# Sixteen of 22 input units as seven half-size products each (Strassen), in two passes over K, with the combinations and all stages through DRAM

## The chip, the cores and the metric

The kernel runs on one core of a Trainium2 chip. The metric is the time of the whole execution on the device in microseconds, the median over several runs of the same program. All tensors come from DRAM and the result goes back to it. Everything below is float32; a product of two float32 matrices is made from rounded high parts and remainders, as told below.

## The reference, cut to what matters

One pre-norm mixer layer of a hybrid encoder on x of 1024 tokens and 2048 columns:

```python
h = rmsnorm(x, norm_w)                       # 1024 x 2048
proj = einsum('bsd,de->bse', h, w_in)        # 2048 x 5632 input weights
q_a, k_a, v_a, g_a, q_r, k_r, v_r, g_r = split(proj)
# widths: 1024, 256, 256, 1024,  512, 512, 1024, 1024
attn = windowed_attention(q_a, k_a, v_a, sink, rel_bias)   # 16 heads of 64, 4 KV heads, +-128 tokens
attn = rmsnorm(attn, attn_out_norm_w) * silu(g_a)
ret = bidirectional_retention(rotary(q_r), rotary(k_r) * 64**-0.5, v_r, ...)   # 8 heads, chunks of 128
ret = head_groupnorm(ret, ret_gn_w) * silu(g_r)
x = x + einsum('bse,ed->bsd', concat(attn, ret), w_out)    # 2048 x 2048
return rmsnorm(x, final_norm_w)
```

The two projections are most of the arithmetic. Attention looks at bands of three 128-token blocks, with a learned sink and a relative-position bias; retention runs a scan over chunks of 128 tokens in each direction.

## The kernel before, in words

**Products.** [...] A product is three matmuls into one accumulator: high by high, high by low, low by high.

**Units.** The 5632 input columns are cut into 22 units of 256 columns, named for what they hold: "ka" and "va" (attention keys and values), four each of "qa" (queries), "ga" and "gr" (gates of attention and retention), "qk" (retention queries and keys) and "vr" (retention values). A unit takes 16 k-steps of 128 rows of the 2048; a step multiplies into four accumulators "psM" of 128 columns by 512 tokens (L817 to L819, 128x512 matmuls). In "va" and "vr" the result is wanted with tokens on the partitions: eight 128x256 products a step (L810 to L812). So a unit is 192 wide matmuls, or 384 of half the width. The normalised input lies in SBUF as hT, 32 rows of 128x1024: for each k-step a high and a low row. It holds x times the norm weight; the factor 1/rms per token is put on when an accumulator is taken out (evac, with the tile "rb" or the column "rcol").

**Weights.** One transfer of 256 KB brings two k-steps ("wr", two buffers). ScalarE casts the high part "wh" (L105), GpSimd subtracts for the low part "wl" (L99; VectorE in the output phase). Each has two buffers, and a pair feeds 24 matmuls.

**Side work.** After each three matmuls point() may advance two queues of generators: `jobs` holds attention (160 steps, in four groups) and retention (four jobs of two heads), `aux` the set-up: sums of squares, the bias rows, decay factors, gates and rotary factors after their units. The bias rows are copied by DMA sixteen times from "br" to "bd" through the shared tiles t (t2, 6 buffers), right after they have been computed. Attention and retention results go to DRAM "md", gates after their tanh to "gd"; before the output projection mixed_row loads a row, scales it and splits it into hT.

**Output.** Eight units (two halves of the tokens, four blocks of 512 columns) multiply hT by w_out, 192 matmuls each (L899 to L901); the last has its weights in the free part of hT already.

**Order.** The program emits instructions as these loops run, and a scheduler then sets the order on each engine, so an engine's order is read from the compiled program. An engine works off its own order and waits on semaphores. All loads and stores are issued by SyncE (SP), each one only after the one eight places earlier has landed.

## Time and profile before

| | us |
|---|---|
| time, median of 3 runs (lowest, highest) | 1581.26 (1580.31, 1585.71) |
| the profiled execution: its time | 1581.46 |
| its span, first instruction to last | 1579.7 |
| TensorE busy | 1539.7 (97%) |
| VectorE busy | 798.9 (51%) |
| ScalarE busy | 525.2 (33%) |
| GpSimd busy | 414.1 (26%) |
| bytes over DMA | 171.76 MB, mean 109 GB/s |

Mean granted TensorE clock 0.994 of full speed.

Engines are named PE (TensorE), DVE (VectorE), ACT (ScalarE), POOL (GpSimd) and SP (SyncE, which issues transfers). A row of the view by stretches is: the stretch in us after the span's start and its length; busy us of PE (and number of matmuls, as x192), then of the weight loads of PE, of DVE, ACT and POOL; the granted TensorE clock as a share of full speed; the mean busy share of the 16 DMA engines and the GB/s they moved. A row of the groups is: line, engine, operation, output tile and inputs, shape, count | busy us, mean ns of one | idle us of the engine right before them, and which instruction's end finished most of that idle time. A row of the chain of waits is a time, a length and the work that released the next. A row of the DMA issues ends with the KB of one and the median us from issue to landing. "PE psT L502 <- DVE PTl L99: 4.0, 9, 1.2" in the view of waits is: who waits for whom, us in all, how often, the longest.

A busy TensorE is the usual state of this program. The input units run from 6.2 to 1216.7 us, the output units from there to 1570; the rest is the last rows' norm and stores.

### The profile page before, as it was taken

What the parts mean: (1) busy time and instruction counts of PE and PEld (TensorE: products, weight loads), DVE (VectorE), ACT (ScalarE), POOL (GpSimd) and SP (SyncE); (2) the same over time, 40 slices, a digit from 0 to 9 for tenths busy, and PEclk for the clock granted to TensorE, in tenths of its full rate; (3) what the DMA queues carried; (4) which work ended last, traced back from release to release, by engine and by line L of the source; (5) the groups of instructions that cost most, each with busy time, mean ns of one, the idle gap of its engine ahead of it and who ended that gap; (6) DMA issues with size and microseconds to landing.
All of it is one profiled execution on the core that took longest, in us unless ns stands there. A gap on an engine that the chain in (4) does not pass through costs nothing.

```text
span 1579.7 us, 22620 instructions
## 1 busy us (share of the span) xinstructions
PE 1539.7 (97%) x8338; PEld 1327.6 (84%) x8338; DVE 798.9 (51%) x1888; ACT 525.2 (33%) x1186; POOL 414.1 (26%) x435
## 2 busy tenths in 40 slices
PE   8979999999999999999999999999999999999997
PEld 6968888888888888888998998998988888888886
DVE  5511156644656478466534825735567463463323
ACT  5412145543554356456410111111123243433310
POOL 2212223332334334334331423323322000320000
PEclk9989999999999999999999999999999999999999
DMA  8774313131213123212231321312222565675423
GB/s 299 246 248 125 104 43 92 51 114 45 84 56 114 48 60 94 73 48 83 54 113 41 107 61 50 111 41 67 88 89 91 186 205 151 180 247 139 127 61 113
DMA packets 111020, 171.76 MB, mean 109 GB/s; under 512 B 17932, under 2 KB 39436, under 8 KB 110781
## 3 DMA queue, kind: packets, MB, share of 16 engines
q1 hardware_dynamic: 110908, 170.32, 35.3%
q8 instruction: 65, 1.06, 0.3%
q14 instruction: 47, 0.38, 0.1%
HBM read 138.26 MB, written 32.01 MB: 108 GB/s over the span
## 4 chain that ended last, share of the span: by engine, by line
PE 82%; DVE 8%; DMA 4%; issue 3%; ACT 1%; POOL 1%; SPq 0%; POOLq 0%; ACTq 0%; DVEq 0%
PE psM L817 14%; PE psM L818 14%; PE psM L819 14%; PE psM L811 3%; PE psM L812 3%; PE psM L810 3%; PE psM L900 3%; PE psM L901 3%; PE psM L899 3%; PE psT L502 2%; DMA t<-br 1%; DVE t L102 1%; PE psS L900 1%; PE psS L899 1%; PE psS L901 1%
## 5 line engine op out<-in xcount | busy, mean ns | idle before, releaser
L817 PE MATMUL psM<-hT,wh 128*128 128x512 f32 x1088 | 443.0, 407 | 14.9 <-ACT t L741 8.7
L819 PE MATMUL psM<-hT,wl 128*128 128x512 f32 x1088 | 425.9, 392 | 2.0 <-POOL wl L99 2.0
L818 PE MATMUL psM<-hT,wh 128*128 128x512 f32 x1088 | 426.2, 392 | 0.0
L99 POOL TENSOR_TENSOR wl<-wr,wh 128x512 fp32r<-128x512 f32 x176 | 234.5, 1333 | 583.7 <-ACT wh L105 570.7
L105 ACT CAST wh<-wr 128x512 fp32r<-128x512 f32 x288 | 178.5, 620 | 568.7 <-PE psM L818 226.4
L817 PEld LDWEIGHTS psM<-hT,wh 128*128 128x128 f32 x1088 | 205.7, 189 | 53.6 <-ACT t L741 8.9
L819 PEld LDWEIGHTS psM<-hT,wl 128*128 128x128 f32 x1088 | 204.9, 188 | 47.3 <-POOL wl L99 2.4
L818 PEld LDWEIGHTS psM<-hT,wh 128*128 128x128 f32 x1088 | 206.1, 189 | 37.5 <-DVE hT L102 0.7
L810 PE MATMUL psM<-wh,hT 128*128 128x256 f32 x640 | 183.5, 287 | 1.4 <-ACT wh L105 1.4
L811 PE MATMUL psM<-wl,hT 128*128 128x256 f32 x640 | 181.9, 284 | 2.4 <-POOL wl L99 2.4
L812 PE MATMUL psM<-wh,hT 128*128 128x256 f32 x640 | 181.8, 284 | 0.0
L99 DVE TENSOR_TENSOR wl<-wr,wh 128x512 fp32r<-128x512 f32 x112 | 84.1, 751 | 130.8 <-ACT wh L105 130.7
L811 PEld LDWEIGHTS psM<-wl,hT 128*128 128x128 f32 x640 | 123.4, 193 | 3.0 <-POOL wl L99 2.8
L810 PEld LDWEIGHTS psM<-wh,hT 128*128 128x128 f32 x640 | 123.5, 193 | 2.5 <-ACT wh L105 1.6
L812 PEld LDWEIGHTS psM<-wh,hT 128*128 128x128 f32 x640 | 123.4, 193 | 0.0
L450 DVE CUSTOM_DVE_ANT_0 P<-psS,bias,nsink 128x384 f32<-128x384 f32 (+1 forms) x128 | 74.3, 580 | 91.7 <-PE psS L444 91.3
L454 ACT ACTIVATE P<-P,nmx 128x384 f32<-128x384 f32 (+1 forms) x128 | 75.6, 590 | 92.1 <-DVE nmx L450 90.7
L900 PE MATMUL psM<-wl,hT 128*128 128x512 f32 x256 | 100.0, 391 | 0.6 <-DVE wl L99 0.5
L899 PE MATMUL psM<-wh,hT 128*128 128x512 f32 x256 | 100.0, 391 | 0.0
L901 PE MATMUL psM<-wh,hT 128*128 128x512 f32 x256 | 99.7, 389 | 0.0
L99 POOL TENSOR_TENSOR acc<-acc,sq 64x128 f32<-64x128 f32 x112 | 54.9, 490 | 156.2 <-ACT sq L483 148.1
L99 DVE TENSOR_TENSOR t<-psM,rb 128x512 f32<-128x512 f32 x64 | 42.2, 685 | 93.4 <-PE psM L819 93.2
(200 smaller groups left out, 2259.6 us busy)
## 6 DMA issues: line engine op xcount, KB each, us to landing
wr<-in_w_in SPq DMA_DIRECT2D x176, 256.0 KB, 2.7
wr<-in_w_out SPq DMA_DIRECT2D x112, 256.0 KB, 2.8
t<-in_x SPq DMA_DIRECT2D x16, 512.0 KB, 6.9
mr<-md SPq DMA_DIRECT2D x32, 256.0 KB, 3.0
xr<-in_x SPq DMA_DIRECT2D x32, 256.0 KB, 3.9
out<-y SPq DMA_DIRECT2D x32, 256.0 KB, 3.0
t<-in_xT SPq DMA_DIRECT2D x15, 512.0 KB, 5.8
gd<-t SPq DMA_DIRECT2D x28, 256.0 KB, 2.4
```

Source lines behind the costliest of these rows:

```text
L99: eng.tensor_tensor(o, x, y, op)
L105: A.copy(o_hi, x)
L454: A.activation(x[:, :W], x[:, :W], AF.Exp, bias=nmx[:, c : c + 1], scale=-1.0, accum_out=sums[:, c : c + 1])
L810: T.matmul(po, hh[:, sl], wh[:, ws], start=first and z == 0, stop=False, skip_group_check=True)
L811: T.matmul(po, hh[:, sl], wl[:, ws], start=False, stop=False, skip_group_check=True)
L812: T.matmul(po, hl[:, sl], wh[:, ws], start=False, stop=last, skip_group_check=True)
L817: T.matmul(p, wh[:, ws], hh[:, sl], start=first, stop=False)
L818: T.matmul(p, wh[:, ws], hl[:, sl], start=False, stop=False)
L819: T.matmul(p, wl[:, ws], hh[:, sl], start=False, stop=last)
L899: T.matmul(p, mh, wh, start=(k == 0), stop=False)
L900: T.matmul(p, mh, wl, start=False, stop=False)
L901: T.matmul(p, ml, wh, start=False, stop=(k == NK - 1))
```

## The change

**Sixteen units as Strassen products.** "ka", "va" and the four "qa" stay as they were and come first (STD). The other sixteen (FAST) are taken as block products in Strassen's form with Winograd's sums: K is cut into two passes of 1024 rows, and in each pass a unit's weights (1024 x 256) and the input (1024 tokens) are seen as 2x2 blocks. Seven products of half-size blocks replace eight, so a unit and pass takes 7 x 4 x 3 = 84 matmuls of 128x512 (L953 to L955) instead of 96. No unit of FAST has tokens on the partitions now: "vr" is transposed afterwards, four 128x128 transposes a block, 64 in all (L1035).

**The input's combinations.** The seven left-hand combinations of the input are the same for all units. combine() makes them in the side queue during the standard units: it loads blocks of x again, normalises them fully, forms sums, splits each into a tile "crow" (128x1024, two buffers) and stores it to DRAM "cd", 28 rows of 512 KB for each pass. Standard units still use the first form of hT. The 28 rows of the first pass are loaded into hT during the last standard unit (whose k-steps run 14, 15, 0 to 13, so that rows come free early), those of the second when the pass changes.

**The weights' combinations.** w_fast holds the weights in blocks. prep() loads four 256 KB blocks for a unit and pass, VectorE forms two sums and GpSimd two more, and each of the seven is split as before (ScalarE cast, GpSimd low part) two products ahead of its use, with three buffers for each part.

**The results' combinations.** Products accumulate in "psMa" and "psMb", two banks each. collect() copies the partial sums of bank a out between products that go on adding to it, by ScalarE in the first pass and VectorE in the second. The first pass's four results of a unit go to DRAM "yd" and come back to be added in the second. deliver() then makes the gates, rotary products or token-order values of a result and stores them to DRAM, from where retention and mixed_row load them.

**What else moves.** Queries are split and staged through DRAM "qsd" for attention. Copies of the bias rows are cut in groups of four: the first stands behind combine(0) in the side queue, three in the last standard unit. The gates are multiplied in mixed_row, for eight of the sixteen rows with one more operation on GpSimd. A step of attention or retention is taken each 3.1 calls of point(), later each 4.2 (before: 3), and one of the side queue each 2.0, later 2.4 (before: 2).

```diff
+STD = [("ka", 0), ("va", 0), ("qa", 0), ("qa", 1), ("qa", 2), ("qa", 3)]
+FAST = []
 for _p in range(4):
-    UNITS += [("qk", _p), ("vr", _p)]
+    FAST += [("qk", _p), ("vr", _p)]
+FAST += [(_k, _p) for _k in ("ga", "gr") for _p in range(4)]
...
+    def combine(ph):
+        for j in range(4):
+            b = [stp.tile([128, 512], F32, tag=f"b{x}", name=nm("b"), bufs=1) for x in range(4)]
+            for x in range(4):
+                k = 8 * ph + 4 * (x // 2) + j
+                SP.dma_start(b[x], a["xT"][k][:, 512 * (x % 2) : 512 * (x % 2) + 512])
+            yield
+            yield
+            for x in range(4):
+                k = 8 * ph + 4 * (x // 2) + j
+                stt(V, b[x], b[x], nw[:, k : k + 1], rb[x % 2], ALU.mult, ALU.mult)
+            b11, b12, b21, b22 = b
+            def row(p, t):
+                c = stp.tile([128, 1024], F32R, tag="crow", name=nm("crow"), bufs=2)
+                split(c[:, 0:512], c[:, 512:1024], t, G if p % 2 else V)
+                SP.dma_start(cd[ph, 4 * p + j], c.bitcast(F32))
+            row(0, b11)
+            yield
+            tt(V, b11, b12, b11, ALU.subtract)
+            row(3, b11)
+            yield
...
+    aux.append((combine(0), None))
+    aux.append((bias_copies(0), None))
+    aux.append((combine(1), None))
+    aux.append((decay(), None))
...
+            k = (pos + 14) % NK if last_u else pos
...
+            if last_u and pos >= 4:
+                for r in range(2 * pos - 8, 2 * pos - 6):
+                    c_load(0, r)
...
+    def prep(q, p):
...
+        elif p == 2:
+            s1, s2 = rt(F32), rt(F32)
...
+            tt(V, s1, w(2), w(3), ALU.add)
+            tt(V, s2, s1, w(0), ALU.subtract)
+            src = s2
...
+        hi, lo = wpair(q)
+        split(hi, lo, src, G)
...
+    def multiply(q, p):
+        if p in (0, 1, 3):
+            banks[q, "abc"[(0, 1, 3).index(p)]] = psum("Ma" if p == 0 else "Mb", 2)
+        bank = banks[q, {0: "a", 2: "a", 4: "a", 5: "a", 1: "b", 3: "c", 6: "c"}[p]]
...
+        for j in range(4):
...
+            hh, hl = hT[:, 4 * p + j, 0:512], hT[:, 4 * p + j, 512:1024]
+            T.matmul(bank, wh[:, ws], hh, start=(j == 0 and p in (0, 1, 3)), stop=False, skip_group_check=True)
+            T.matmul(bank, wh[:, ws], hl, start=False, stop=False, skip_group_check=True)
+            T.matmul(bank, wl[:, ws], hh, start=False, stop=(j == 3), skip_group_check=True)
+            point()
+    def partial(q, b):
+        if (q, b) not in outs:
+            outs[q, b] = et_(("e11", "e12", "e21", "e22")[b])
+            if q >= NF:
+                SP.dma_start(outs[q, b], yd[q - NF, b])
+        return outs[q, b]
+    def collect(q, p):
...
+        def take(b, bank):
+            o = partial(q, b)
+            if ph:
+                tt(V, o, bank, o, ALU.add)
+            else:
+                A.copy(o, bank)
+            return o
+        if p == 0:
+            take(0, ba)
+        elif p == 1:
+            tt(V, outs[q, 0], bb, outs[q, 0], ALU.add)
+            deliver(q, 0)
+        elif p == 2:
+            take(1, ba)
...
+    for q in range(2 * NF):
+        slots.append((q, 0))
+        if q:
+            slots.append((q - 1, 5))
+        slots.append((q, 1))
+        if q:
+            slots.append((q - 1, 6))
+        slots += [(q, 2), (q, 3), (q, 4)]
...
+    for n, (q, p) in enumerate(slots):
+        if n + 2 < len(slots):
+            prep(*slots[n + 2])
...
+        multiply(q, p)
...
+        collect(q, p)
...
+        if old:
+            pp = old.popleft()
+            for j in range(4):
+                c_load(1, 4 * pp + j)
+        if q == NF - 1:
+            old.append(p)
```

Three places show how instructions moved. Rows name the line, the operation, the output tile and its inputs, and the shape; "x2" stands for two in a row.

ScalarE in the standard units, before: behind the two copies of "rb" (the 1/rms factors) its weight casts "wh" follow one another, with a few small set-up operations.

```order
L130 COPY rb<-psS_660 128x512
L130 COPY rb<-psS_666 128x512
L304 ACTIVATE lu_1029<-lz_1030 128x24
L105 CAST wh_741<-wr_676 128x512
L318 ACTIVATE cdec<-lg_1033 128x16
L321 ACTIVATE kdec<-kdec 128x16
L105 CAST wh_807<-wr_745 128x512
L105 CAST wh_873<-wr_811 128x512
```

The same engine there in the changed program; "crow" are the combined rows, "b" the blocks they are cast from, "e" the tiles that now hold raw weights.

```order
L120 CAST crow_804<-b_756 128x512
L120 CAST wh_837<-e_111_774 128x512
L120 CAST crow_827<-b_756 128x512
L120 CAST crow_850<-b_757 128x512
L120 CAST crow_867<-b_756 128x512
L120 CAST wh_909<-e_116_841 128x512
L337 ACTIVATE lu_2092<-lz_2093 128x24
L120 CAST crow_889<-b_759 128x512
L120 CAST crow_905<-b_758 128x512
L120 CAST wh_976<-e_123_913 128x512
```

Two or three casts of combined rows now stand ahead of each weight cast.

SP in the middle of attention, before: one weight load at a time, between the attention's stores and loads.

```order
L143 DMA wr_4133<-in_w_in 128x512
L493 DMA md<-u_4077 64x2x128
L509 DMA gt_4182<-gd 64x2x128
L143 DMA wr_4202<-in_w_in 128x512
L493 DMA md<-u_4168 64x2x128
L509 DMA gt_4264<-gd 64x2x128
L143 DMA wr_4281<-in_w_in 128x512
```

SP at the end of the last standard unit, in the changed program; "r" are the raw weight blocks of the first products.

```order
L465 DMA qj_2941<-qsd 64x2x256 x2
L544 DMA md<-u_2951 64x2x128
L810 DMA hT<-cd 128x1024 x2
L286 DMA bd<-t_494_2925 128x512
L909 DMA r_3010<-in_w_fast 128x512
L909 DMA r_3012<-in_w_fast 128x512
L909 DMA r_3014<-in_w_fast 128x512
L909 DMA r_3016<-in_w_fast 128x512
L810 DMA hT<-cd 128x1024 x4
L909 DMA r_3039<-in_w_fast 128x512
L909 DMA r_3041<-in_w_fast 128x512
```

The first products' weights stand behind 24 row loads of hT, and the bias copies to "bd" are now among them.

ScalarE in the densest attention, before:

```order
L513 CAST PTh_3895<-psT_3932 128x3x128
L454 ACTIVATE P_3923,sums_3870<-P_3923,nmx_3869 128x384
L457 ACTIVATE esk_3871<-esk_3871 128x2
L105 CAST wh_3948<-wr_3861 128x512
L454 ACTIVATE P_3966,sums_3964<-P_3966,nmx_3963 128x256
L479 COPY sq_3982<-psO_3974 64x256
L513 CAST PTh_3994<-psT_3990 128x3x128
```

The same engine in the first pass of the changed program; "e" are partial sums taken out of "psMa".

```order
L507 ACTIVATE P_4555,sums_4506<-P_4555,nmx_4505 128x256
L510 ACTIVATE esk_4507<-esk_4507 128x2
L977 COPY e_905_4573<-psMa_4211 128x512
L120 CAST wh_4577<-r_4306 128x512
L532 COPY sq_4605<-psO_4597 64x256
L507 ACTIVATE P_4594,sums_4592<-P_4594,nmx_4591 128x384
L536 ACTIVATE sq_4605<-u_4604 64x256
L560 CAST PTh_4615<-psT_4612 128x2x128
L120 CAST wh_4627<-r_4296 128x512
L977 COPY e_920_4625<-psMa_4581 128x512
```

A weight cast stands there for each product of 12 matmuls, and copies of the banks stand between them.

668 lines of the change are left out of this document (395 added, 273 removed).

## The prediction

> **What bounds the kernel now.** I read the head of the page first, then its chain of waits, then busy time in stretches cut at the boundaries of units.
>
> ```profile
> span 1579.7 us, 22620 instructions
> PE 1539.7 (97%) x8338; PEld 1327.6 (84%) x8338; DVE 798.9 (51%) x1888; ACT 525.2 (33%) x1186; POOL 414.1 (26%) x435
> PE 82%; DVE 8%; DMA 4%; issue 3%; ACT 1%; POOL 1%; SPq 0%; POOLq 0%; ACTq 0%; DVEq 0%
> ...
> 160.49:204.01 43.52, 43.52 (x193) 36.04 (x192) 5.96 (x9) 8.31 (x15) 10.33 (x8) 1.00 0.31 94
> 1308.41:1351.93 43.52, 43.52 (x194) 36.04 (x193) 15.80 (x25) 13.61 (x27) 0.00 (x0) 1.00 0.48 130
> 935.19:994.34 59.15, 59.05 (x314) 49.44 (x313) 31.14 (x83) 6.87 (x12) 15.97 (x15) 1.00 0.18 55
> 994.34:1044.03 49.69, 49.69 (x417) 49.58 (x416) 25.64 (x63) 6.97 (x12) 15.78 (x11) 1.00 0.29 90
> 52.20:114.40 62.20, 51.19 (x404) 49.59 (x402) 20.04 (x51) 12.56 (x26) 11.88 (x9) 0.93 0.69 224
> 114.40:160.50 46.10, 46.10 (x192) 37.91 (x193) 8.36 (x29) 10.02 (x26) 10.31 (x8) 0.94 0.47 138
> ```
>
> TensorE is 82% of the chain. The first two stretches are one input unit and one output unit: 192 matmuls of 128x512 in 43.52 us, nothing lost, at full clock (1.00). So a matmul costs 0.2267 us, and the 30 units' worth (22 input, 8 output) cost 1305.6 of the span's 1579.7 us. The other 274.1 us are the attention and retention matmuls between them, the start, the tail, and one loss: the unit "va" (52.2 to 114.4) leaves TensorE idle for 11.0 us, and half-clock time makes the next unit 2.6 us long (46.10 against 43.52).
>
> **The floor of the change.** Sixteen input units become 2 passes x 16 units x 7 products x 12 matmuls = 2688 of the same 128x512 form, against 16 x 192 = 3072: two units fewer, 87.0 us. The loss in "va" goes:
>
> ```profile
> 84.37 5.39 DMA t<-br
> ...
> 108.70 4.60 DMA bd<-t
> 113.48 0.85 ACT t L741 x2
> 114.37 0.80 PE psM L817
> ...
> L652 PE MATMUL psT<-ident,on 128*128 128x128 f32 x64 | 9.9, 275 | 0.0
> ```
>
> These chain pieces show it: the evacuation waits for buffers that the copies of the bias rows hold. The change queues these copies behind the first combinations, so 11.0 + 2.6 = 13.6 us go. Added are 64 transposes of the values "vr" to token order; the same number of retention transposes (last row, of the groups by line) is busy 9.9 us. Against that, four "vr" units drop their 256-wide matmuls: 994.34 to 1044.03 has 49.69 us with 32 small retention matmuls, which at 0.13 us each (15.6 us over 43.52 for some 121 of them in 935.19 to 994.34) are 4.2, leaving 1.9 over 43.52, 7.6 for four. Floor: 1579.7 - 87.0 - 13.6 + 9.9 - 7.6 = 1481.4 us, if nothing new makes TensorE wait. Attention and retention keep their matmuls.
>
> **What the change adds, and what hides it.** The transfers of the program grow from 170.3 to 314.5 MB, counted from the rows of the order. These are the rates and latencies to hold against it:
>
> ```profile
> 6.20:52.20 46.00, 45.96 (x192) 37.19 (x193) 27.00 (x29) 26.24 (x31) 11.58 (x8) 1.00 0.92 332
> 30.00:45.00 15.00, 15.00 (x68) 12.43 (x67) 7.33 (x9) 8.68 (x11) 4.51 (x3) 1.00 0.96 343
> 45.00:60.00 15.00, 15.00 (x99) 13.75 (x97) 8.88 (x12) 6.80 (x12) 2.58 (x2) 1.00 0.98 343
> 1340.00:1395.00 55.00, 55.00 (x245) 45.53 (x244) 23.40 (x25) 24.04 (x45) 19.38 (x15) 1.00 0.61 182
> ...
> gd<-t SPq DMA_DIRECT2D x28, 256.0 KB, 2.4
> t<-in_xT SPq DMA_DIRECT2D x15, 512.0 KB, 5.8
> wr<-in_w_in SPq DMA_DIRECT2D x176, 256.0 KB, 2.7
> ...
> DMA to landing us min/median/max: 2.9/4.1/5.3
> ...
> L105 ACT CAST wh<-wr 128x512 fp32r<-128x512 f32 x288 | 178.5, 620 | 568.7 <-PE psM L818 226.4
> L99 POOL TENSOR_TENSOR wl<-wr,wh 128x512 fp32r<-128x512 f32 x176 | 234.5, 1333 | 583.7 <-ACT wh L105 570.7
> L99 DVE TENSOR_TENSOR wl<-wr,wh 128x512 fp32r<-128x512 f32 x112 | 84.1, 751 | 130.8 <-ACT wh L105 130.7
> L99 DVE TENSOR_TENSOR t<-psM,rb 128x512 f32<-128x512 f32 x64 | 42.2, 685 | 93.4 <-PE psM L819 93.2
> ```
>
> The stretches are in us, with the DMA engines' share and GB/s at the end; the issues show the median us to landing. The queues are full at 343 GB/s (shares 0.96 and 0.98).
>
> *Combinations, standard units, +18.* In the order, ScalarE casts 56 rows "crow" among 28 weight casts. A weight tile feeds 24 matmuls, 5.44 us, so a row has 2.72 us before TensorE waits: the weight cast stands behind it in ScalarE's order. A row needs its cast (0.62), the low part (0.75 on VectorE for four of seven, 1.33 on GpSimd for three, mean 1.0, 1.1 with a semaphore or two) and its 512 KB store. There are two buffers. The only 512 KB store in the trace is that of rbd; that tile's three transfers landed after 2.9, 4.1 and 5.3 us, and 4.1 is the middle one: (0.62 + 1.1 + 4.1) / 2 = 2.9 us a row, 0.18 x 56 = 10 us late. Lower bound: landing after 2.4 us (gd<-t, half the size), nothing late. Upper bound: 5.8 us (t<-in_xT, in a full queue), 3.76 us a row, 58 us late. The same stretch of SP's order moves 51.9 MB in 28 x 5.44 = 152 us of TensorE work, and at 343 GB/s that takes 151 us. A queue that may never pause, on which stores wait for compute, will pause: I add 8, for 18 in all.
>
> *Into the first pass, +5.* During the last standard unit SP's order holds 22.0 MB, 64 us at 343 GB/s. The unit is 43.5 us plus 24 attention steps at 0.8, 62.9 us (0.8: in 204 to 772 stand ten units, 435 of 568 us; less the idle 6.1 shown below, 127 us for some 157 steps). The first product's weights are queued behind 24 row loads and need 2.7 + 0.62 + 1.33 us more, of which two positions of the unit, 7.8 us, give cover. Bounds 0 and 12 (cover gone); 5 lies nearer the queue's own 1 us.
>
> ```profile
> 204.00:480.00 276.00, 273.56 (x1377) 232.57 (x1377) 156.63 (x413) 130.70 (x341) 94.33 (x111) 1.00 0.25 70
> 480.00:655.30 175.30, 172.57 (x883) 145.08 (x881) 107.79 (x274) 88.30 (x234) 69.07 (x90) 1.00 0.29 81
> 655.30:772.00 116.70, 115.79 (x598) 98.98 (x598) 77.19 (x209) 62.94 (x168) 42.19 (x54) 1.00 0.21 62
> ...
> PE psT L502 <- DVE PTl L99: 4.0, 9, 1.2
> ```
>
> *First pass, +8.* Before, TensorE idles 2.4 + 2.7 + 0.9 us through all of attention, and the longest wait for a low part there is 1.2 us (last row's third number). Now one bank of four partial sums is copied out between products, twice per unit with a single product (2.72 us and its share of attention) between copy and next write: 32 spots. VectorE goes from 107.8 / 175.3 = 61% to at most 88% (9 steps x 2.2, from 341.6 us in 157 steps with all evacuations, plus five ops at 0.7, in 19.0 + 7.2 us). Bounds 0 and 32 x 1.2 = 38; a quarter of a microsecond per spot is 8. The weight splits (0.62, then 1.33) run two products ahead and stay covered; without that cover each product would be 2 us late.
>
> *Between passes, +10.* All 28 rows of hT are loaded again, 19.7 MB from the first to the last row load in SP's order: 57 us at 343 GB/s, against 16 products with what is left of attention, 43.5 + 12.6 = 56 us. But a product's rows cannot be asked for before it is done, so in the first three slots only one seventh of it can be on its way: some 8 us of rate lost. Bounds 0, and 25 at 298 GB/s (182 / 0.61, the 2 KB rows of the fourth line above) with that loss.
>
> *Second pass, +10.* VectorE now takes the copies itself (13 ops a unit or less beside ropes), each after a reload of its partial sum, while retention runs: 56.8 us per job (31.14 + 25.64, ropes in it) over 4.2 units, 13.5, plus 6.3, in 19.0 + 5.2 us: 82%. Same 32 spots, same bounds, a little more.
>
> *Last products, +4.* Fourteen rows of mixed input are split there by VectorE (0.75 and one more op each), some 21 us in 24.5 us that also hold retention; before, a whole unit covered it. Bounds 0 and 15.
>
> Sum: 18 + 5 + 8 + 10 + 10 + 4 = 55, so a span of 1536. The profiled execution took 1581.46 us with its span of 1579.7, 1.8 more, and lies 0.2 from the median of the runs, 1581.26. Forecast: **1538 us**.
>
> [...]
>
> **The rivals.** *The transfers keep ahead:* row loads and stores that have no compute behind them overlap, store landings are nearer 2.4 than 4.1, and only waits for banks and the last products stay, 4 + 5 + 4: 1481.4 + 13 + 1.8 = 1496. For it: 332 GB/s were held through the first unit (6.20 to 52.20) with TensorE busy. Against it: those were loads into five buffers, not stores from two. [...]
>
> *No change:* the two passes are bound by banks and VectorE; 32 spots at about 1 us in each pass, 30 + 35, with the other terms as above (37): 1481.4 + 102 + 1.8 = 1585. For it: 82 to 88% on an engine that serves in order. Against it: the densest attention before, at 61%, lost 2.7 us in 175.
>
> *Slower:* one mechanism, the two-buffer store of combined rows inside the standard units. If a 512 KB store lands as the 512 KB loads did at the start, 5.8 us, the term is 58, and the same full queue gives both passes' row loads their upper bounds, 12 and 25: with 8 + 10 + 4, 1481.4 + 117 + 1.8 = 1600. With those loads it decides from (98.3 - 59) / 56 = 0.70 us over 2.72, a row cycle of 3.4 us, which is a landing of 5.1 us.
>
> That the change doesn't do what it says I exclude: the order holds the 2688 matmuls.
>
> **How the numbers follow.** Forecast 0.50 (its own range 1515 to 1562), transfers ahead 0.22, no change 0.12, slower 0.16. A difference of 0.3%, 4.7 us, is what these runs can tell. Of "no change" I give 0.04 to faster, 0.06 to same, 0.02 to slower. Faster 0.76, same 0.06, slower 0.18. The range of 1488 to 1595 holds the forecast and no change whole and most of the first rival (1488 is 5 over the floor's 1483), and leaves out slower.
>
> **What would show it.** For the floor: a fast product without attention in 2.72 us, and the gap in "va" gone. For the combinations: the page's GB/s near 300 through the standard units, casts of "crow" idle behind its store, and units there some 6 us over 43.5. For the passes: two dips in TensorE, at the last standard unit and in the middle of the products. Waits of TensorE on ScalarE (first pass) or VectorE (second) before the third and fifth product would be the bank spots. Wrong is the forecast if store landings stay under 3 us, if the longest waits stand in the passes' steady part, or if fast products run well over 2.72 us without a wait.

## The result: slower by 7%, and the profile after

The changed kernel takes 1691.86 us (median of 4 runs, 1689.79 to 1698.35), the kernel before 1582.98 beside it: a ratio of 1.0695, 95% interval 1.0659 to 1.0731. The forecast was 1538, its range 1488 to 1595. The profiled execution took 1689.79 us with a span of 1688.0.

The head of the page of the changed kernel, and its chain of waits by engine:

```profile
span 1688.0 us, 22276 instructions
PE 1513.9 (90%) x7250; PEld 1242.1 (74%) x7250; DVE 1040.6 (62%) x2082; ACT 636.4 (38%) x1368; POOL 663.9 (39%) x587
...
PE 40%; DVE 19%; DMA 12%; POOL 9%; issue 7%; ACT 5%; SPq 2%; POOLq 0%; ACTq 0%; DVEq 0%
```

The matmuls did become fewer: 7250 rows for 8338, though TensorE's busy time fell by only 26 us. TensorE was 82% of the chain and is 40%; VectorE, transfers and GpSimd have taken its place.

Busy time in stretches of the changed kernel, cut at the five standard units before the last, the last standard unit, the first pass, the first three units of the second, the rest of it to its last unit, that unit with the first output unit, and the other output units. The expectations below call the units of both passes f0 to f31 and the output units o0 to o7: the first pass is f0 to f15, the joint of the passes f16 to f18, and f19 to f31 is the second pass up to its last unit.

```profile
6.50:273.40 266.90, 237.76 (x1171) 198.86 (x1171) 151.37 (x219) 94.24 (x156) 90.03 (x64) 0.95 0.78 272
273.40:369.50 96.10, 76.77 (x339) 57.87 (x340) 47.34 (x143) 42.43 (x117) 14.60 (x17) 0.90 0.93 305
369.50:829.30 459.80, 422.58 (x2145) 349.96 (x2144) 318.81 (x731) 262.71 (x667) 244.31 (x255) 1.00 0.44 134
829.30:911.80 82.50, 72.90 (x328) 58.72 (x327) 45.99 (x66) 19.33 (x36) 53.13 (x42) 0.92 0.80 277
911.80:1264.10 352.30, 311.35 (x1549) 255.94 (x1548) 259.44 (x532) 87.19 (x146) 193.56 (x148) 0.96 0.47 149
1264.10:1367.30 103.20, 84.79 (x382) 69.34 (x382) 71.11 (x155) 31.92 (x55) 27.92 (x21) 0.87 0.66 217
1367.30:1678.40 311.10, 307.69 (x1345) 251.31 (x1343) 142.24 (x231) 94.22 (x188) 37.29 (x31) 1.00 0.54 169
```

Held against the prediction's floor of 1481.4 us: a unit is 43.52 us there ("ka" 46.0, "va" 51.2, its gap taken off), a unit and pass of seven products 84 x 0.2267 = 19.04, and the 236.7 us left between start and tail go evenly over 1664 matmuls of attention, retention and transposes, 0.142 each.

| stretch | measured | floor | over | forecast |
|---|---|---|---|---|
| five standard units | 266.9 | 227.8 | 39 | 18 |
| last standard unit (147 small matmuls) | 96.1 | 64.4 | 32 | 5 |
| first pass (799) | 459.8 | 418.2 | 42 | 8 |
| joint of the passes (74) | 82.5 | 67.6 | 15 | 10 |
| second pass to its last unit (540) | 352.3 | 305.3 | 47 | 10 |
| last unit and first output unit (104) | 103.2 | 77.3 | 26 | 4 |
| seven output units | 311.1 | 304.6 | 6 | 0 |

Sum over: 207, where 55 were forecast. No stretch was forecast too high.

Two more views carry the search. TensorE's waits, of the changed kernel:

```profile
PE psT L553 <- DVE PTl L114: 33.0, 35, 2.3
PE psMa L953 <- DVE e L114: 30.5, 12, 5.9
PE psMa L887 <- DVE t L114: 11.7, 3, 6.3
PE psO L682 <- DVE ST L117: 10.6, 5, 3.7
PE psMa L887 <- ACT wh L120: 8.8, 5, 5.3
PE psMa L887 <- ACT t L797: 7.6, 1, 7.6
PE psO L528 <- DVE PTl L114: 7.5, 13, 1.6
```

The first is attention's one transpose bank, waiting for VectorE to read it, and the last a matmul that needs what VectorE reads there: 36.7 us of both lie in the first pass, where TensorE is idle for 37.2. The second is the bank of partial sums. The L887 rows are standard units: "DVE t" and "ACT t" are waits for a bank that has not been taken out, "ACT wh" for a weight cast. The stall of 7.6 us, at the end of "va", in the chain of waits:

```profile
106.33 4.32 DMA cd<-crow
110.76 0.62 ACT crow L120
111.37 0.75 ACT t L797 x2
112.12 0.75 PE psMa L887
```

The two copies that empty the bank ("t") stand on ScalarE behind the cast of a combined row, which waits for the store of an earlier row to free its tile. And the granted clock (the third number from the end) around two stalls:

```profile
210.53:213.94 3.41, 1.38 (x7) 0.80 (x5) 3.12 (x2) 1.42 (x3) 3.08 (x3) 1.00 0.91 366
213.94:220.77 6.83, 4.05 (x10) 3.22 (x11) 6.83 (x9) 2.85 (x5) 2.76 (x2) 0.50 0.51 169
220.77:224.18 3.41, 3.41 (x17) 2.80 (x16) 1.45 (x3) 0.68 (x2) 0.00 (x0) 1.00 0.91 320
...
930.74:934.15 3.41, 1.52 (x10) 1.39 (x11) 3.15 (x5) 0.00 (x0) 1.26 (x1) 1.00 0.25 77
934.15:937.56 3.41, 3.41 (x10) 2.65 (x9) 0.00 (x0) 0.00 (x0) 0.00 (x0) 0.50 0.01 2
```

The first stall is one gap of 4.8 us, of which 2.0 lie in the first stretch; 6.8 us at half clock follow. The second is one gap of 2.2 us (1.9 of them in its stretch), and 3.4 us at half clock follow. A 128x512 matmul starts every 0.43 us in that stretch at half clock (934.15 to 937.56), for 0.2267 at full clock. So a stall was paid for twice here: ahead of the tail there are some 119 us at half clock in 19 places, each 3.41 us long or two or four times that, which is up to 60 us of lost work, about 43 if TensorE's idle time inside them is left out. On the grid of these stretches 17 of the 19 follow one with 1.88 us of idle time or more, and after TensorE's first matmul none with more than 1.89 us was followed by full clock. Before there were 13.7 us at half clock, all around the gap in "va".

### The profile page after: what moved, and what is told of

It is laid out like the page before. It is cut to its first block, busy times and chain, and to the rows that moved or that the text cites. A ratio compares the mean times of both kernels' runs of the same rounds, so it can differ in the third digit from the quotient of the medians.

```text
span 1688.0 us, 22276 instructions
## 1 busy us (share of the span) xinstructions
PE 1513.9 (90%) x7250; PEld 1242.1 (74%) x7250; DVE 1040.6 (62%) x2082; ACT 636.4 (38%) x1368; POOL 663.9 (39%) x587
## 4 chain that ended last, share of the span: by engine, by line
PE 40%; DVE 19%; DMA 12%; POOL 9%; issue 7%; ACT 5%; SPq 2%; POOLq 0%; ACTq 0%; DVEq 0%
POOL wl L114 4%; PE psMa L953 4%; PE psMa L954 4%; PE psMa L955 4%; DMA cd<-crow 2%; DVE e L114 2%; DVE ST L117 2%; DVE P L515 2%; PE psMb L953 2%; PE psMb L955 2%; PE psMb L954 2%; DVE P L503 2%; PE psT L553 1%; DVE PTl L114 1%; POOL r L114 1%
## 5 line engine op out<-in xcount | busy, mean ns | idle before, releaser
L114 POOL TENSOR_TENSOR wl<-r,wh 128x512 fp32r<-128x512 f32 x224 | 299.3, 1339 | 233.7 <-ACT wh L120 217.8
L953 PE MATMUL psMa<-hT,wh 128*128 128x512 f32 x512 | 218.6, 427 | 35.0 <-DVE e L114 30.5
L120 ACT CAST wh<-r 128x512 fp32r<-128x512 f32 x224 | 137.8, 617 | 280.5 <-PE psMa L954 161.6
L955 PE MATMUL psMa<-hT,wl 128*128 128x512 f32 x512 | 206.8, 404 | 0.4 <-POOL wl L114 0.3
L954 PE MATMUL psMa<-hT,wh 128*128 128x512 f32 x512 | 206.9, 404 | 0.0
L120 ACT CAST wh<-e 128x512 fp32r<-128x512 f32 x160 | 98.4, 619 | 163.4 <-PE psMb L1155 69.3
L953 PE MATMUL psMb<-hT,wh 128*128 128x512 f32 x384 | 158.5, 413 | 0.0
L955 PE MATMUL psMb<-hT,wl 128*128 128x512 f32 x384 | 151.2, 394 | 0.7 <-POOL wl L114 0.7
L954 PE MATMUL psMb<-hT,wh 128*128 128x512 f32 x384 | 150.6, 392 | 0.0
L953 PEld LDWEIGHTS psMa<-hT,wh 128*128 128x128 f32 x512 | 100.6, 196 | 58.4 <-issue 25.6
L955 PEld LDWEIGHTS psMa<-hT,wl 128*128 128x128 f32 x512 | 100.3, 196 | 24.4 <-POOL wl L114 1.2
L954 PEld LDWEIGHTS psMa<-hT,wh 128*128 128x128 f32 x512 | 101.0, 197 | 17.4
L114 POOL TENSOR_TENSOR r<-r,r 128x512 f32<-128x512 f32 x64 | 87.8, 1372 | 41.9 <-DVE r L114 35.6
L887 PE MATMUL psMa<-hT,wh 128*128 128x512 f32 x140 | 59.3, 423 | 34.4 <-DVE t L114 11.1
L114 DVE TENSOR_TENSOR r<-r,r 128x512 f32<-128x512 f32 x64 | 56.9, 889 | 48.4 <-POOL wl L114 32.9
```

The source lines that it names most:

```text
L114: eng.tensor_tensor(o, x, y, op)
L120: A.copy(o_hi, x)
L887: T.matmul(p, wh[:, ws], hh, start=first, stop=False)
L953: T.matmul(bank, wh[:, ws], hh, start=(j == 0 and p in (0, 1, 3)), stop=False, skip_group_check=True)
L954: T.matmul(bank, wh[:, ws], hl, start=False, stop=False, skip_group_check=True)
L955: T.matmul(bank, wl[:, ws], hh, start=False, stop=(j == 3), skip_group_check=True)
```

## The experiments

Each is the changed kernel with one edit, unless it says otherwise, and is read by the stretches above. All but the last four are one execution each. Eight of them leave the standard units as they were, and the five units took 263 to 268 us there, so a difference of some 4 us in such a stretch tells nothing.

**Standard units: what stalls at their ends?**

Two buffers for each block of x in combine(), then four for the combined rows:

```diff
-stp.tile([128, 512], F32, tag=f"b{x}", name=nm("b"), bufs=1)
+stp.tile([128, 512], F32, tag=f"b{x}", name=nm("b"), bufs=2)
```

> Edit: the four tiles of combine() that hold blocks of x get two buffers each instead of one, so a set is loaded while the set before is still being combined. Theory 'order' (TensorE stalls because bank evacuations stand on VectorE and ScalarE behind combination steps that wait for a load or a store): VectorE's idle time before the block normalisation, 25 us in the standard units, falls under 5; two of the four stalls at unit ends (those near 163 and 213 us) go with their half-clock stretch, and the five units from 6.5 to 273.4 us (266.9) take 10 to 18 us less. Rival 'bytes' (the stretch is bound by the transfers): the same bytes, the five units within 3 us of 266.9. Rival 'row stores' (the two-buffer store of combined rows, as the prediction had it): also within 3 us.

1691.97 us. VectorE's idle time before the normalisation fell from 30.8 to 7.1 us as each theory has it, and "qa0" from 51.9 to 46.3, but the fifth unit grew from 56.6 to 71.3: five units 269.3. The wait was there, the gain was not: the time went to waits elsewhere (VectorE for GpSimd's low part of a row, which is the row minus its cast, 30.6 us for 18.1). By its time alone this run is what the two rivals forecast; the next ones speak against them.

```diff
-c = stp.tile([128, 1024], F32R, tag="crow", name=nm("crow"), bufs=2)
+c = stp.tile([128, 1024], F32R, tag="crow", name=nm("crow"), bufs=4)
```

> Edit: the tile of combined rows gets four buffers instead of two. Theory 'order': of the four stalls in the standard units the one at the end of the unit va (7.6 us, whose chain goes through a row's store) and part of the one near 244 us go; the five units take 8 to 15 us less than 266.9. Rival 'row stores': the row cycle is halved and nearly all of the 39 us over the floor goes: 25 us or more less. Rival 'bytes': within 3 us.

1681.39 us, five units 258.8, which is 8 less than in the changed kernel's profile and 4 to 9 less than in the runs that leave them alone; "va" fell from 58.6 to 53.4. So the two-buffer store, which was the forecast's mechanism, is a part of the loss, but not the 25 us or more that it would have been as the whole. The row of the issues in the changed kernel fits:

```profile
cd<-crow SPq DMA_DIRECT2D x56, 512.0 KB, 3.0
```

A row lands after 3.0 us in the median (2.6 to 6.6), not 4.1 or 5.8: (0.62 + 1.1 + 3.0) / 2 = 2.4 us a row, within its 2.72. A late row can still cost time, as at the end of "va" (4.32 us, above). Without any combination:

```diff
-for j in range(4):
+for j in ():                                   # in combine()
-SP.dma_start(hT[:, r, :].bitcast(F32), cd[ph, r])
+SP.dma_start(hT[:, r, :].bitcast(F32), qsd[(r % 12) // 2, r % 2])
```

> Edit: the combinations of the input are left out: no blocks of x are loaded, summed, split or stored in the standard units, and the rows of hT are loaded from rows of the split queries in DRAM, as many bytes as before. Theory 'order': without combination steps on VectorE, ScalarE, GpSimd and SP nothing holds up the evacuations and weight loads at the unit ends: qa0 to qa2 take 43.5 to 45 us each (51.9, 52.7, 56.6 in the changed kernel) and the stretch to 273.4 us is 25 to 35 us shorter. The last standard unit (96.2 us) stays over 80 if its row loads set it. Rival 'weights' (the standard units' raw weights now go through two shared tiles and come late by themselves): qa0 to qa2 stay over 48.

Stretches of that run, the five units and one of them:

```profile
6.40:232.60 226.20, 225.45 (x1170) 193.19 (x1171) 72.89 (x125) 64.07 (x109) 57.65 (x42) 1.00 0.52 170
...
102.10:145.60 43.50, 43.50 (x194) 36.01 (x193) 9.72 (x28) 10.11 (x26) 10.26 (x8) 1.00 0.38 108
```

All 39 us are the combinations': the five units fall to 226.2, a unit to 43.50. Their transfers are gone too (170 GB/s for 272), so this run does not tell their work from their bytes. The last standard unit falls to 70.7 as well, but the first pass takes 475.5 us, 16 more, of which the 21 small matmuls that moved into it explain 3; the whole is 1649.71.

All three waits removed at once (combined rows in a tag of five buffers with their low parts on VectorE, two buffers for each block, and the small decay loads issued early):

```diff
+    aux.append((decay_loads(), None))          # right behind bias_rows()
-split(c[:, 0:512], c[:, 512:1024], t, G if p % 2 else V)
+split(c[:, 0:512], c[:, 512:1024], t, V)
```

> Edit, alone on the changed kernel: only what happens in the standard units: combined rows go through a tag of five buffers and their low parts all to VectorE, blocks of x have two buffers, and the small loads of the decay factors are issued behind the bias rows, long before their use, instead of right ahead of it (in the run with five edits one evacuation waited 15.3 us behind them). Theory 'order': with the three waits for stores, block loads and the decay loads gone together, the five units take 228 to 245 us (266.9; 226.2 without combinations). Rival 'amount' (the combinations' work itself is too much for VectorE and the queues): 255 or more.

1674.69 us, five units 249.4: between the two readings. 17 of 39 us went with these waits and with the low parts' move, at the same bytes; the other 22 stay, with TensorE still waiting for an evacuation on VectorE (5.3 us once) and casts on ScalarE (4.1 and 4.2). Whether these 22 are the combinations' work or their bytes (296 GB/s in this stretch) no run tells.

**The two passes: banks, order, or GpSimd?**

The two weight sums of VectorE moved to GpSimd:

```diff
-tt(V, s1, w(2), w(3), ALU.add)
-tt(V, s2, s1, w(0), ALU.subtract)
+tt(G, s1, w(2), w(3), ALU.add)
+tt(G, s2, s1, w(0), ALU.subtract)
```

> Edit: the two weight sums that VectorE makes for each unit and pass are made by GpSimd, which already makes the other two. Theory 'order': VectorE waits 25.7 us in the first pass, in order, for GpSimd and for weight loads before these sums, and spends 28.6 us on them; attention's copies out of the one transpose bank stand behind them (TensorE waits 29.8 us for those). The first pass (369.5 to 829.3, 459.8 us) takes 15 to 30 us less, the second 5 to 20 less. Rival 'GpSimd': its busy share rises from some 53% to 65% or more in the first pass and weights come late: the first pass the same or up to 15 us longer, with waits of TensorE on low parts. Rival 'banks' (only the copies between products count): within 4 us.

1700.04 us; first pass 461.6, second 364.6 (352.3). VectorE was freed of 28.6 us of work and 25.7 of waiting, and nothing came of it: its busy time in the first pass fell by only 9.0 us (318.8 to 309.8), since other operations grew. That is the rival 'GpSimd' in time, but without the waits on low parts that it named. The groups of the first pass show which ones grew. Scaling of P, the sink's sum, and an operation that reads a bank; before, in the changed kernel, and in this run:

```profile
L462 DVE TENSOR_SCALAR P<-P,sums 128x384 f32<-128x384 f32 (+1 forms) x110 | 54.9, 541 | 1.7
L99 DVE TENSOR_TENSOR esk<-nmx,sink 128x2 f32<-128x2 f32 x55 | 15.2, 276 | 1.4
L99 DVE TENSOR_TENSOR PTl<-psT,PTh 128x384 fp32r<-128x384 f32 (+1 forms) x106 | 55.4, 522 | 32.1 <-ACT PTh L513 28.6
```

```profile
L515 DVE TENSOR_SCALAR P<-P,sums 128x384 f32<-128x384 f32 (+1 forms) x107 | 69.3, 688 | 1.8
L114 DVE TENSOR_TENSOR esk<-nmx,sink 128x2 f32<-128x2 f32 x53 | 30.1, 568 | 1.2
L114 DVE TENSOR_TENSOR PTl<-psT,PTh 128x384 fp32r<-128x384 f32 (+1 forms) x107 | 55.9, 523 | 33.2 <-ACT PTh L560 31.4
```

```profile
L515 DVE TENSOR_SCALAR P<-P,sums 128x384 f32<-128x384 f32 (+1 forms) x107 | 83.8, 823 | 1.8
L114 DVE TENSOR_TENSOR esk<-nmx,sink 128x2 f32<-128x2 f32 x53 | 31.8, 600 | 1.5
L114 DVE TENSOR_TENSOR PTl<-psT,PTh 128x384 fp32r<-128x384 f32 (+1 forms) x107 | 56.0, 523 | 39.2 <-ACT PTh L560 36.8
```

In these three, the more GpSimd works (36% of attention's stretch before, 53% in the first pass, 62% here), the longer take P's scaling (541, 688, 823 ns) and the sink's sum (276, 568, 600 ns), whose operands lie in SBUF; the one that reads a bank stays at 522 or 523 ns. Not every operation in SBUF grows: the reciprocal of the row sums stays at 165 or 166 ns. That GpSimd's work is what holds the two up is the theory 'port' below; through what in the chip it would do so, no run shows.

The copies between products left out, so that a unit and pass takes four results out of its banks instead of seven:

```diff
-if p == 0:
-    take(0, ba)
-elif p == 1:
-    tt(V, outs[q, 0], bb, outs[q, 0], ALU.add)
+if p == 1:
+    take(0, bb)
```

> Edit: the copies of a bank between the products that go on adding to it are left out, so a unit and pass takes four results out instead of seven (the sums are not the block products then). All matmuls, loads, stores and weight sums stay. Theory 'banks': the second pass has 24.7 us of TensorE waits for these copies in ten places and most of its half-clock stretches follow them; it takes 30 to 45 us less (829.3 to 1295.4, 466 us), the first pass, where no such wait is seen, 0 to 10 less. Theory 'order' says the same of the second pass, and 5 to 15 us for the first, since VectorE has one operation less in each unit. Rival 'bytes' or plain load of retention: under 10 us in the second pass.

1673.60 us: first pass 457.6, joint 72.3, second pass 351.0. The joint gives 10 us, the steady parts 2 and 1, where both theories had 30 to 45 for the joint and the second pass. Of the 24.7 us of waits at these banks 8.6 lay in the joint. Those in the second pass were not the banks' own: without them TensorE still waits 36.9 us for VectorE there, at other places, for 40.9 in the changed kernel.

GpSimd out of the products (its sums and the weights' low parts left out, so that the result is not the product):

```diff
-split(hi, lo, src, G)
-ready_w[q, p] = (hi, lo)
+A.copy(hi, src)
+ready_w[q, p] = (hi, hi)
```

> Edit: in the products GpSimd does nothing: its two weight sums and the low parts of the weights are left out (the third matmul reads the high part instead), so the result is not the product. VectorE's two sums, all casts, copies, loads, stores and matmuls stay. Theory 'port' (a VectorE operation whose operands both lie in SBUF, or that only scales a tile in SBUF, is held up while GpSimd works; the scaling of P went from 541 ns before to 685 here and 818 with the sums on GpSimd, the sums of the sink from 276 to 568 to 600, while operations that read PSUM stayed, 522, 523, 523): the scaling goes back to 540 or less, the first pass (459.8 us) takes 25 to 40 us less, and f19 to f31 of the second (352.4) 15 to 30 less. Rival 'order': VectorE's waits for these buffers go too (19.6 us for GpSimd in the first pass), so 5 to 15 less in each. Rival 'bytes' or plain load: within 5 us in both passes.

1579.76 us, 112 less. First pass and second pass of that run:

```profile
368.40:781.50 413.10, 412.99 (x2146) 351.75 (x2145) 255.05 (x731) 262.18 (x667) 52.02 (x108) 1.00 0.48 149
...
853.40:1157.30 303.90, 298.38 (x1550) 249.50 (x1549) 217.06 (x531) 87.74 (x146) 48.50 (x40) 0.99 0.54 172
```

That is more than any theory had. TensorE is idle for 0.1 us in the first pass, and both passes lie at their floor or just under it (418.2 and 305.3), with every transfer, bank copy and cast still in place. VectorE's same 731 operations take 255.05 us in place of 318.81. That run takes away both GpSimd's work and the waits for its results. Dummies of the same shape, whose results nobody reads, tell them apart in part (ScalarE's next cast still waits for a dummy that reads its tile, 4.1 us in the first pass):

```diff
 A.copy(hi, src)
+tt(G, scr, hi.bitcast(F32), hi.bitcast(F32), ALU.subtract)
 ready_w[q, p] = (hi, hi)
```

> Edit: as in the run without GpSimd in the products, but GpSimd does an operation of the same shape on tiles in SBUF in place of each one left out (nine for each unit and pass), whose result nobody reads and for which neither VectorE nor the weight loads wait; the result is not the product. It tells two readings of that run apart, in which the first pass fell to 413.0 us and f19 to f31 to 303.9. Theory 'port': GpSimd's work as such stretches VectorE's operations in SBUF; they are as long as in the changed kernel (scaling of P 0.65 us or more) and most of the loss is back: first pass 440 to 460, f19 to f31 335 to 355. Theory 'order' (VectorE, the raw buffers and the matmuls wait for GpSimd's results): without those waits first pass 413 to 421, f19 to f31 304 to 312, whatever the durations.

1628.08 us:

```profile
368.00:796.80 428.80, 419.09 (x2146) 352.36 (x2145) 289.34 (x732) 264.09 (x667) 213.32 (x254) 0.99 0.46 143
874.00:1206.10 332.10, 306.60 (x1549) 253.66 (x1548) 249.38 (x532) 87.66 (x146) 170.70 (x148) 0.97 0.49 157
```

Between the theories: (428.8 - 413.1) of 46.7 us come back in the first pass, a third, and (332.1 - 303.9) of 48.4 in the second, 58%. So much is GpSimd's mere work, in a dose of 0.87 of the real one. The rest, but for the smaller dose, goes with waiting for its results: in the changed kernel VectorE's weight sums stand 25.7 us in its order, 19.6 of them for GpSimd to free a buffer; with the dummies 1.5.

The low parts on VectorE instead, so that the products stay what they are:

```diff
-split(hi, lo, src, G)
+split(hi, lo, src, V)
```

> Edit: the low parts of the products' weights are made by VectorE instead of GpSimd, which keeps two weight sums; the result is the same. Theory 'port': GpSimd's busy share falls from 53% to about 30% in the first pass, VectorE's operations in SBUF shrink (scaling of P under 0.6 us), and though VectorE takes 0.75 us for each of seven more operations in a unit (some 82 us in the first pass) it ends up near 75 to 82% busy: first pass 420 to 445 us against 459.8, f19 to f31 320 to 345 against 352.4. Rival 'load' (VectorE is simply at its limit): first pass 460 or more. Theory 'order': 435 to 455, the waits for GpSimd gone but those for the casts behind VectorE's other work in their place.

1621.96 us, 70 less, with VectorE busier than ever:

```profile
363.70:786.50 422.80, 415.82 (x2146) 351.94 (x2144) 333.72 (x845) 262.60 (x668) 108.10 (x141) 1.00 0.46 145
860.90:1193.40 332.50, 307.70 (x1549) 254.03 (x1548) 283.27 (x617) 87.60 (x146) 80.82 (x64) 0.97 0.49 158
```

79% in the first pass, and 37 us shorter than at 69%. VectorE's load was not the matter. Scaling the attention weights P by the row sums (69.3 us of VectorE in the first pass) on ScalarE instead, with the same result:

```diff
-V.tensor_scalar(y[:, :W], y[:, :W], sums[:, cc : cc + 1], None, ALU.mult)
+A.activation(y[:, :W], y[:, :W], AF.Copy, scale=sums[:, cc : cc + 1])
```

> [...] Theory 'port': this operation is the one that GpSimd stretches most on attention's chain (685 ns against 541 before); ScalarE does it in about 0.6 us, VectorE has 15% of the first pass more free: the first pass takes 15 to 30 us less than 459.8 and the transposes' waits for VectorE (29.3 us) halve. Rival 'order on ScalarE': ScalarE's casts of the weights and P's exponentials now stand behind this scaling, the first pass within 5 us or longer.

1676.66 us, first pass 446.7: 13 less. Joined with low parts on VectorE (the run with five edits, below) it gained nothing over them: there ScalarE is busy 325 of 450 us.

**The last standard unit and the last products.** No row loads:

```diff
-SP.dma_start(hT[:, r, :].bitcast(F32), cd[ph, r])
+pass
```

> Edit: the loads of the combined rows into hT are left out in both places, 56 transfers of 512 KB, so the products read what lies in hT (old values). All else stays. Theory 'bytes' for the two joints: the last standard unit (96.2 us, against some 64 of TensorE work) falls to 64 to 75, and the joint of the passes (82.4) to 70 to 75. Theory 'order': attention's start and the combinations' end hold the last unit up anyway, it stays over 85, and the joint at 78 or more.

1662.45 us. The last standard unit falls from 96.1 to 65.9 (with 110 small matmuls for 147, 7 us over its floor of 59.2), the joint from 82.5 to 77.3. The bias copies alone, moved behind that unit:

```diff
-for g in range(1, 4):                          # in the last standard unit
-    aux.append((bias_copies(g), None))
+for g in range(1, 4):                          # behind it
+    aux.append((bias_copies(g), None))
```

> Edit, alone on the changed kernel: the copies of bias groups 1 to 3 (24 transfers of 256 KB, 6.3 MB) are put into the side queue behind the last standard unit instead of at its start. Reading 'bytes' of the last standard unit (leaving out its row loads took it from 96.2 to 65.9 us, the run with five edits from 96.2 to 61.1): 6.3 MB are some 18 us of full queues, the unit falls to 75 to 85 us. Reading 'weights' (its raw weights, 5.3 us from issue to landing, stand behind those copies and row loads in SP's order): to under 75. Reading 'combinations' (their end holds it up): over 90.

1674.24 us, the unit 81.0: 15 less. Of the 6.3 MB 4.7 had moved in that stretch (18 transfers), which are 15 us at its 305 GB/s. With queues at a share of 0.93, bytes were the matter here.

**Together.** Five edits at first (low parts on VectorE in the first pass and for four of seven products in the second, scaling on ScalarE, the row and block buffers, the bias copies later):

> Edit: five things together, the result is the same: low parts of the products' weights on VectorE in the first pass and for four of seven products in the second; scaling of P on ScalarE; low parts of the combined rows on VectorE, in a tag of five buffers, with two buffers for each block of x; the bias copies of groups 1 to 3 put behind the last standard unit instead of into it. Theory 'port' with the stalls behind combinations: standard units 226 to 250 us (266.9), last standard unit 75 to 88 (96.2), first pass 415 to 435 (459.8), f19 to f31 320 to 345 (352.4): 1560 to 1620 us in all. Rival 'load' on VectorE: first pass 455 or more, and 1650 or more in all.

1624.12 us: five standard units 261.7, last standard unit 61.1, first pass 449.6 with 836 small matmuls (floor 423), second 338.5; one evacuation of the standard units waited 15.3 us behind the decay factors' small loads. Then all low parts on VectorE and P's scaling back there, the standard units' three edits, the bias copies later, the mixed rows a stage earlier, retention's scaled transposes on ScalarE, and:

```diff
+rbA[hf] = com.tile([128, 512], F32, tag="rbA", name=nm("rbA"), bufs=1)    # 1/rms once for each half
-V.tensor_copy(s[64:128, 0:384], q[64:128, 128:512])
+A.copy(s[64:128, 0:384], q[64:128, 128:512])
```

> Edit: low parts of all product weights on VectorE; the bias copies behind the last standard unit; the standard units' buffers and early decay loads; the 1/rms rows for the mixed input loaded once for each half instead of eight times, and each mixed row loaded a stage earlier; retention's copies out of the banks and its scaled transposes on ScalarE in place of VectorE. The result is the same. If the causes found are the whole story they add up: first pass and joint as in the run with low parts on VectorE (422.8 and 74.4), standard units 228 to 245, last standard unit 62 to 75, f19 to f31 315 to 330, f31 to o1 80 to 95: 1540 to 1575 us, below the kernel before. If they hide one another: 1590 or more.

1589.62 us (1587.06 to 1591.86), a ratio to the kernel before of 1.0048 (1.0029 to 1.0067): 102 of the 109 us of the loss are gone, and it is still 0.5% slower. That is outside the 1540 to 1575 of causes that simply add up. Its stretches, standard units to last units:

```profile
6.40:257.50 251.10, 235.20 (x1171) 198.06 (x1172) 159.98 (x239) 93.13 (x155) 63.47 (x42) 0.97 0.84 295
257.50:324.90 67.40, 62.15 (x299) 49.42 (x298) 41.68 (x113) 33.04 (x91) 12.70 (x13) 0.97 0.89 295
324.90:760.50 435.60, 423.48 (x2186) 355.91 (x2185) 341.12 (x880) 271.52 (x694) 108.97 (x143) 1.00 0.51 159
...
837.00:1165.20 328.20, 306.56 (x1550) 253.18 (x1549) 262.66 (x572) 105.86 (x189) 80.07 (x64) 0.97 0.49 160
1165.20:1265.50 100.30, 82.86 (x382) 66.86 (x381) 72.06 (x157) 33.40 (x57) 22.05 (x17) 0.91 0.63 203
```

Three attempts at what was left, on this version, gained nothing. Bank copies of the second pass by ScalarE (`A.copy(z, bank)`, then VectorE adds z):

> Edit: on the joined version, in the second pass the copies of a bank between products are made by ScalarE into a tile of their own, and VectorE adds that tile to the partial sum; the result is the same. In the joined version TensorE waits 16.5 us in eleven places, up to 3.4 us, for VectorE's add out of the bank, and two half-clock stretches follow such waits. Theory 'banks' (with GpSimd out of the way VectorE's order at the copied banks is what is left): these waits fall under 5 us, f19 to f31 takes 10 to 20 us less than 328.2, the whole 1570 to 1580. Rival 'load': VectorE's add is as long from SBUF, its own order is as late for all else, and ScalarE's casts of weights stand behind copies that wait for matmuls: within 5 us of 1589.6 or longer.

1590.04 us (ratio 1.0055, 1.0034 to 1.0076), second pass 328.0. In it TensorE's waits for that bank fell from 6.5 to 1.5 us (in the whole run from 16.5 to 7.9), and those for VectorE elsewhere rose from 15.0 to 19.5. With the side queue held back at unit ends besides, and two smaller things:

> Edit: on the version with ScalarE at the banks, two things: the side queue is not advanced during the last two k-steps of a standard unit (and runs at every 2.0 calls in place of 2.4 elsewhere), so that no new combination step stands ahead of an evacuation; and the low parts of the second half of the mixed rows go to GpSimd. The result is the same. Theory 'order' of the standard units (evacuations wait in order behind combination steps; the five units take 251 us in the joined version, 226.2 without combinations): 8 to 20 us less in these units, if the emission order carries over to the engines' order. Rival 'amount': the steps only move, within 5 us. The output units (314.8 us, against 305.2 before): 0 to 6 less.

1601.38 us (1.0125, 1.0108 to 1.0142): the five units 260.6, where the run before had 247.8, and the seven output units 322.0 for 313.9. With three things changed at once, it says no more than that they gain nothing together. Retention's steps each 3.5 calls instead of 4.2, on the joined version without the last two edits:

> Edit: on the joined version, one step of retention each 3.5 calls in place of 4.2, so that retention ends some two units earlier; the result is the same. Reading 'crowding' of the last products (the last retention job, the mixed rows and the last units' gates share VectorE there; 100.3 us from f31 to o1, 23 over the floor): that stretch falls by 8 to 15 us, f19 to f31 (328.2) grows by what retention it takes over, the sum of both falls by 5 to 12: 1578 to 1585 in all. Rival 'chain' (mixed rows and weights of the output are late by themselves): the sum stays within 4 us.

1598.64 us (1.0094, 1.0065 to 1.0123). In its profile, which is its longest execution (1604.82), f19 to o1 took 437.8 in place of 428.5 us, 9 more, where one reading had 5 to 12 less and the other the same within 4:

```profile
836.60:1178.80 342.20, 324.12 (x1654) 266.97 (x1653) 283.17 (x656) 111.61 (x198) 89.84 (x71) 0.97 0.48 156
1178.80:1274.40 95.60, 70.79 (x277) 55.36 (x276) 54.74 (x75) 28.11 (x48) 19.13 (x14) 0.86 0.69 222
```

The last products and the first output unit take 95.6 us without one retention matmul, against 62.6 of their own: 33 over, where it was 23 with retention among them. So retention's crowding is not what holds them. The chain of waits there goes through the mixed rows (loads of their gates 31% of it, GpSimd's product 10, VectorE's split 8), and TensorE's longest wait, 12.1 us, is for the first output unit's weights.

## Why the prediction was wrong, step by step

- **The floor held.** Matmul counts and times were right: without GpSimd the passes took 413.1 and 303.9 us against 418.2 and 305.3, without combinations a unit 43.50.
- **First and second pass, +8 and +10, were 42 and 47.** This is the step that failed most. It counted operations on VectorE and looked for late ones at the copied banks; VectorE's share stayed under its count (69 and 74% for 88 and 82). It set the splits on GpSimd down as "covered", and for TensorE they were (1.0 us of waits in both passes). So GpSimd's hold on VectorE was put at nothing. But GpSimd's share rose from 36 to 53%; with it P's scaling went from 541 to 688 ns and the sink's sum from 276 to 568, and VectorE's order stood 19.6 us for GpSimd's late results in the first pass: without GpSimd in the products 46.7 and 48.4 us were gone. The trace before had a sign of it: the sink's sum on 128x2 elements took 276 ns there, the reciprocal of as many 165; with GpSimd out of the products the sum takes 157. The bound "32 x 1.2" came from the longest wait before, under a lesser GpSimd.
- **Combinations, +18, were 39**, for the most part by another mechanism: not a row's store cycle (landing 3.0 us) ahead of weight casts, where more buffers gave 4 to 9 us, but evacuations queued on VectorE and ScalarE behind combination steps that wait for a load or a store. They have 2 us of cover, since the next unit writes the first bank again after nine more matmuls (9 x 0.2267). Of the 39 us 17 went when these waits were taken away; what makes the other 22 is not shown.
- **Into the first pass, +5, was 32.** The queues were as full as foreseen (share 0.93), but the sum set 22.0 MB at 343 GB/s against the unit, and 29.3 MB moved in that stretch at 305, with the rest of the combinations and the bias copies among them.
- **Between passes, +10, was 15**; 10 of it went with the bank copies, 5 with the row loads. The size was nearly right, but leaving out the bank copies gave the larger part, not the loads that the term was for. Its upper bound of 25 does not come out of its own numbers: 19.7 MB at 298 GB/s are 66 us, 10 over the 56, and with the 8 some 18; only "slower" used it.
- **Last products, +4, were 26**: the mixed rows' chain of loads, product and split, as far as the last run shows it, not VectorE's 21 us of splitting alone.
- **A term was missing**: the half clock behind a stall, some 43 us, which is counted within the stretches above. The profile before had 13.7 us of it around "va", and the prediction took out the 2.6 us that this cost the next unit without asking what new stalls would cost.
- **Gap in "va" gone: in part.** The bias copies no longer hold it, but a stall of 7.6 us took its place, 4.3 of them a combined row's store.

Of the rivals, "slower" came out nearest in time, and that is luck: its mechanism, rows that land after 5.8 us, was not there; "no change" had the right engine, an in-order VectorE in both passes, with a price of 65 us where 89 were paid, and the wrong reason.

What stays open: 22 us in the standard units, where three removed waits gave 17 and holding the side queue gave none; 26 us of the last products; 23 us of the second pass in the joined version; and how the loss through GpSimd beyond mere work divides between buffers freed late and results awaited.

## What to carry to other kernels

Before work is put on an idle GpSimd, ask which VectorE operations on the critical chain work on tiles in SBUF: look at their mean time at different GpSimd shares (here 276 and 568 ns for the sink's sum, 541 and 688 for P's scaling, at 36 and 53%), since the busy shares alone (69 and 53% here) look harmless. A wait that is removed from an in-order queue is worth little if the next instruction in it is as late (two buffers for each block took 23.7 us off one wait of VectorE, and the five units took 269.3 us for 266.9); leave the whole suspected work out once to learn what it costs, and only then remove its waits one by one. In this kernel a TensorE stall that brought half clock cost about 2 us more than itself (43 us in 19 places).

## What was not expected of the hardware

VectorE's scaling of a 128x384 tile took 401 ns with GpSimd busy for 13% of the stretch, 410 at 26%, 541 at 36% (before), 515 at 50% (dummies), 688 at 53% (the change) and 823 at 62%, while the low part that reads a bank stayed within 521 to 526. The order of 541 and 515 shows that GpSimd's share alone does not set the length; what else does is open. Of the 19 half-clock places ahead of the tail 17 began after a stretch of 3.41 us with 1.88 us of TensorE's idle time or more; the other two began after 0.35 us (at 845.41 us) and 1.54 us (at 1309.62), and what began them is open.
